# A hybrid attention and delta-rule encoder: the last attention norm step moved behind an inverse, four weight splits moved from GpSimd to VectorE

## The chip, the core and the metric

The kernel runs on one NeuronCore of a Trainium2 chip. The metric is the device time of one execution in microseconds (us). The engines are named as in the profile: PE is TensorE's matmuls and PEld its weight loads, DVE is VectorE, ACT is ScalarE, POOL is GpSimd, SP is the engine whose queue issues most transfers; ACT's queue issues some too. Each engine works through its own list of instructions in a fixed order that is set when the program is built.

## What is computed

The reference is a two-layer encoder over 1040 tokens (16 meta tokens and 1024 others) of width 1024. Each layer runs attention and a delta-rule recurrence on the same input, joins their outputs by one projection `w_out`, and goes on with a mixture of experts:

```python
y_att = _mla(...)                       # softmax attention, 4 heads, then an RMS norm per head
out = _rms_norm(out, out_norm.reshape(H_A, V_DIM))
...
def step(S, inp):                       # delta rule, forward and backward, 8 heads of 64
    r_t, w_t, k_t, v_t, kk_t, b_t = inp
    sa = jnp.einsum('bhvk,bhk->bhv', S, kk_t)
    S = S * w_t[:, :, None, :] - sa[..., None] * b_t[:, :, None, :] + v_t[..., None] * k_t[:, :, None, :]
    return S, jnp.einsum('bhvk,bhk->bhv', S, r_t)
...
mixed = jnp.concatenate([y_att, y_rwkv], axis=-1) @ w_out[li]
h = _layer_norm(DN_ALPHA * h + mixed, ln1_g[li], ln1_b[li])
```

## The kernel before

Each of the two layers runs through the same stages: projections, attention, delta rule, router, experts. The change lies at the seam from attention to delta rule, which the profiled execution passes at about 650 us (first layer) and 2260 us (second layer).

Attention ends with `normed` for the last of its four heads (the inner function at L883 to L907). It squares the head's output, sums it by a small matmul (L889), takes a power on POOL (L895), writes the 9x128 factors to DRAM (L897, SP queue), reads them back spread over all partitions as `rs` (L900, SP queue), multiplies (for the last head in one DVE instruction, L906, which waits for `rs`) and stores the normed head to `yatt_d` (L907, a transfer in ACT's queue).

The delta rule (function `rwkv`) cuts the sequence into 17 chunks of 64 and walks forward and backward at once; two steps, one of each direction, are a job. A job has four stages. Stage 0, `grams`, forms products on PE (L1509) that two engines take out of PSUM: `T` by DVE (L1514) and `AA` by ACT (L1515); the PSUM tile `e` has two buffers. Stage 1, `blocks`, inverts 16x16 blocks on DVE in 15 dependent steps of three small instructions (L1550, L1551, L1552), and spreads the result (L1558). Stage 2, `levels`, turns it (L1568, `X`), multiplies on PE (L1578, L1583), corrects and turns again on DVE (L1584, L1585) and finishes with two more products (L1592, L1599) that ACT takes out (L1595, L1602, `Y`). Stage 3, `chain`, is the recurrence: L1640 and L1647 need the state `ring`, L1658 needs `Y`, L1664 forms the next state. The tiles `ring` start as loads on the SP queue (L1611).

Beside this runs the generator `attended`, the projection of attention's output. It loads `w_out` in pieces kc of 128x1024 (L947, SP queue, into the tile `ht` with two buffers) and splits each into `wo_hi` (ACT, L209) and `wo_lo` (L212, on POOL). Then, token tile by token tile, it loads `yraw` from `yatt_d` (L959), splits it into `ya_hi` (ACT) and `ya_lo` (POOL), and runs 24 matmuls (L201 to L203) into PSUM tiles `e`, the same two buffers as stage 0. The order of all instructions on each engine is chosen by the scheduler of the tile framework from the order in which the code issues them; before, the first step of `attended` (the pieces kc 0 to 3) is issued ahead of the first job.

Of the kernel before, what the change touches and what calls it, by code (L numbers as in the profile page):

```python
# [170 lines left out]
def hybrid_encoder(ctx: ExitStack, tc: tile.TileContext, I, out):  # L171
# [184 lines left out]
    for li in range(DEPTH):  # L356
# [378 lines left out]
        with pool(tc, name="at", bufs=1, side="right") as at, pool(tc, name="ate", bufs=1, side="right") as even, \  # L735
# [147 lines left out]
            def normed(hd):  # L883

                sq = wk.tile([128, L], F32, name="p", bufs=5)
                nc.scalar.activation(sq, hd.yatt, AF.Square)
                ps = bank()
                for i, n, col in TILES:
                    nc.tensor.matmul(ps[:n, i:i + 1], sq[:, col:col + n], K("ones")[:, 0:1], start=True, stop=True)  # L889
                t = wk.tile([128, 2, NT + 1], F32, name="rmt")  # L890
                nc.vector.scalar_tensor_tensor(t[:, 0], hd.sums, 1e-6, hd.sums, op0=OP.mult, op1=OP.mult)
                for sl, n in ((slice(0, NT), 128), (slice(NT, NT + 1), META)):
                    nc.vector.scalar_tensor_tensor(t[:n, 0, sl], ps[:n, sl], 1.0 / 128, t[:n, 0, sl], op0=OP.mult,
                                                   op1=OP.add)
                nc.gpsimd.tensor_tensor(t[:, 1], t[:, 0], mhalf.to_broadcast([128, NT + 1]), op=OP.pow)  # L895
                rms_d = dram.tile([NT + 1, 128], F32, name="rms_d", bufs=2)
                nc.sync.dma_start(bass.AP(tensor=rms_d.tensor, offset=rms_d.offset, ap=[[1, 128], [128, NT + 1]]), t[:, 1])  # L897
                rs = wr_.tile([128, L], F32, name="rs", bufs=1)
                for c0, n, at_ in ((META, SEQ, 0), (0, META, SEQ)):
                    nc.sync.dma_start(rs[:, c0:c0 + n],  # L900
                                      bass.AP(tensor=rms_d.tensor, offset=rms_d.offset + at_, ap=[[0, 128], [1, n]]))
                if hd.h < 3:
                    nc.gpsimd.tensor_tensor(rs, hd.yatt, rs, op=OP.mult)
                    nc.gpsimd.tensor_scalar(rs, rs, P("on", hd.h), None, op0=OP.mult)
                else:
                    nc.vector.scalar_tensor_tensor(rs, hd.yatt, P("on", hd.h), rs, op0=OP.mult, op1=OP.mult)  # L906
                nc.scalar.dma_start(yatt_d[hd.h], rs)  # L907

            ahead = None
# [24 lines left out]
                    ahead = u  # L934
                before = hd
            values(ahead)
            normed(ahead.head)
        moe, mix = ExitStack(), ExitStack()
        rt = moe.enter_context(pool(tc, name=f"rt{li}", bufs=1))
        nt = NT if last else NT + 1  # L940
# [1 line left out]
        a_d = dram.tile([L, D], F32, name="a_d", tag="a_d", bufs=2)  # L942
        wo = {}

        def w_out(kc):
            raw = fp.tile([128, D], F32, name="ht", bufs=2)
            nc.sync.dma_start(raw, I["w_out"][li, :, kc])  # L947
            wo[kc] = pair(fp, [128, D], f"wo{kc % 4}")
            split(wo[kc], raw, None, nc.gpsimd)

        def attended(bank):


            for kc in range(4):
                w_out(kc)
            yield
            for i, n, col in TILES[:nt]:
                raw = fp.tile([128, 4, 128], F32, name="yraw")
                nc.sync.dma_start(raw[:, :, :n], yatt_d[:, :, col:col + n].rearrange("a p t -> p a t"))  # L959
                ya = pair(fp, [128, 4, 128], "ya")  # L960
                split(ya[:, :, :n], raw[:, :, :n], None, nc.gpsimd)
                ht = fp.tile([128, D], F32, name="ht", bufs=2)
                nc.sync.dma_start(ht[:n], h_rows[2 * li][row0(i):row0(i) + n])
                for j in range(2):
                    js = slice(j * 512, (j + 1) * 512)
                    ps = bank()
                    for kc in range(4):
                        mm3(ps[:n], ya[:, kc, :n], wo[kc][:, js], start=kc == 0, stop=kc == 3)
                    nc.vector.scalar_tensor_tensor(ht[:n, js], ht[:n, js], ALPHA, ps[:n], op0=OP.mult, op1=OP.add)
                    if j == 1:  # L970
                        nc.sync.dma_start(a_d[row0(i):row0(i) + n], ht[:n])
                    yield
            for kc in range(4, 8):
                w_out(kc)
            yield

            while True:
                if not ready:
                    yield
                    continue  # L980
                i = ready.pop(0)
                _, n, col = TILES[i]
                ya = pair(fp, [128, 4, 128], "ya")
                split(ya[:, :, :n], yTr[:, :, col:col + n], None, nc.gpsimd)
                ht = fp.tile([128, D], F32, name="ht", bufs=2)
                nc.sync.dma_start(ht[:n], a_d[row0(i):row0(i) + n])
                for j in range(2):
                    js = slice(j * 512, (j + 1) * 512)
                    ps = bank()
                    for kc in range(4):  # L990
                        mm3(ps[:n], ya[:, kc, :n], wo[4 + kc][:, js], start=kc == 0, stop=kc == 3)
                    nc.vector.scalar_tensor_tensor(ht[:n, js], ht[:n, js], 1.0, ps[:n], op0=OP.mult, op1=OP.add,
                                                   accum_out=sums[:n, i, j:j + 1])
                    if j == 1:
                        nc.sync.dma_start(a_d[row0(i):row0(i) + n], ht[:n])
                        done.append(i)
                    yield
# [1 line left out]
        ready, done = [], []  # L999
        sums = fp.tile([128, NT + 1, 2], F32, name="sums")  # L1000
        yTr = mix.enter_context(pool(tc, name="yr", bufs=1)).tile([128, 4, L], F32, name="yTr")
        finished, finish = rwkv(tc, li, last, K, P, pc, kr_d, bk_d, bon_d, g_dram, vt_d, yTr, mhalf, mix, attended, ready)

        tiles = [TILES[i] for i in finished]
        y_dst = y_rows[li]
# [440 lines left out]
                        tokens(e + 4)  # L1446


def rwkv(tc, li, last, K, P, pc, kr_d, bk_d, bon_d, g_dram, vt_d, yT, mhalf, kept, side, ready):

    nc = tc.nc
    V = nc.vector
# [79 lines left out]
    def blocks(As, E):  # L1532

        n = sum(A.shape[1] for A in As)
        dg = ws.tile([128, n, 16], F32, name="dg")
        at = []
        for A in As:
            U = A.shape[1]
            at.append(slice(at[-1].stop if at else 0, (at[-1].stop if at else 0) + U))
            tmp = ws.tile([128, U, 64], F32, name="tmp")  # L1540
            E.tensor_tensor(tmp, A, K("dg")[:, None, :].to_broadcast([128, U, 64]), op=OP.mult)
            E.tensor_tensor(tmp[:, :, 0:32], tmp[:, :, 0:32], tmp[:, :, 32:64], op=OP.add)
            E.tensor_tensor(dg[:, at[-1]], tmp[:, :, 0:16], tmp[:, :, 16:32], op=OP.add)  # L1543
        Y16 = ws.tile([128, n, 16], F32, name="Y16")
        V.tensor_copy(Y16, K("i16")[:, None, :].to_broadcast([128, n, 16]))
        sb = ws.tile([128, n, 16], F32, name="sb")
        for t_ in range(15, 0, -1):
            cs = slice(t_, 16)
            w = 16 - t_
            V.stream_shuffle(sb[:, :, cs], Y16[:, :, cs], [t_] * 16 + [16 + t_] * 16)  # L1550
            V.tensor_tensor(sb[:, :, cs], sb[:, :, cs], dg[:, :, t_:t_ + 1].to_broadcast([128, n, w]), op=OP.mult)  # L1551
            V.tensor_tensor(Y16[:, :, cs], Y16[:, :, cs], sb[:, :, cs], op=OP.subtract)  # L1552
        Ys = []
        for s in at:
            U = s.stop - s.start
            Y = wk.tile([128, U, 64], F32, name="Y", bufs=4)
            bd = K("bd16")[:, None, :].to_broadcast([128, U, 64])
            V.tensor_tensor(Y.rearrange("p c (b j) -> p c b j", b=4), Y16[:, s, None, :].to_broadcast([128, U, 4, 16]),  # L1558
                            bd.rearrange("p c (b j) -> p c b j", b=4), op=OP.mult)
            Ys.append(Y)  # L1560
        return Ys

    def levels(A, Y):

# [7 lines left out]
        for q0 in range(0, U, 8):  # L1572
# [9 lines left out]
                for s in HALF:  # L1582
                    nc.tensor.matmul(ps[s, u], W[s, q0 + u], Y[s, q0 + u], start=True, stop=True)  # L1583
            V.tensor_tensor(Y[:, q], Y[:, q], ps[:, :nq], op=OP.subtract)  # L1584
        V.transpose(X.rearrange(flat), Y.rearrange(flat))  # L1585

        cf, cg = slice(0, 32), slice(32, 64)
        fg = [(slice(base, base + 32), slice(base + 32, base + 64)) for base in (0, 64)]
# [11 lines left out]
                                 tile_position=(g.start, f.start))  # L1600
        for f, g in fg:
            nc.scalar.activation(Y[f, :, cg], ps[f, :U], AF.Copy, scale=-1.0)  # L1602

    orders = [list(range(NC)), list(range(NC - 1, 0 if last else -1, -1))]
    rings, touched, ends = {}, {}, []
# [114 lines left out]
    def stage(k, j):  # L1720
        if j < len(jobs):
# [4 lines left out]
            elif k == 1:  # L1726
                js = [0] if j == 0 else [x for x in (j, j + 1) if j % 2 and x < len(jobs)]
                if js:
                    Ys.update(zip(js, blocks([gs[x][1] for x in js], V if j == 0 else nc.gpsimd)))
            elif k == 2:  # L1730
                levels(gs[j][1], Ys[j])
            else:
                chain(job, gs.pop(j), Ys.pop(j))

    side = side(lambda: pe.tile([128, 512], F32, name="e"))
    next(side)
    for k, j in ((0, 0), (1, 0), (0, 1), (2, 0), (0, 2), (1, 1)):
        stage(k, j)
        if k == 0 and j == 1:
            for x in range(AHEAD):  # L1740
                new_ring(*steps[x])
# [34 lines left out]
```

## Time and profile before

| | us |
|---|---|
| median of 3 runs | 3237.86 |
| lowest and highest run | 3231.32, 3243.92 |
| profiled execution, its own time | 3243.99 |
| its span in the trace | 3242.1 |

The span is what the trace covers; 1.9 us of the execution's time lie around it, and the profiled execution is 6.1 us above the median. In the timeline rows below, the first number is the start in us from the span's start, the second the duration in us, then engine, line, operation, tiles and count; a bracket at the end holds the idle time of that engine just before the row and what ended it. In the trace a float32 matmul counts as two instructions.

### The profile page before, as it was taken

Reading aid. Unit: us, or ns where it says so; the run is one execution under the profiler, and the core shown is the slowest. Engines: PE = TensorE matmul, PEld = TensorE weight load, DVE = VectorE, ACT = ScalarE, POOL = GpSimd, SP = SyncE. Lnnn points to the kernel's source line nnn. Section 1 sums busy time; section 2 is a strip of 40 time slices with the busy share of each in tenths; the row PEclk is TensorE's granted clock in tenths of the full one; section 3 lists DMA queues with packets and bytes.
Section 4 is the critical chain, followed back from the end, with each engine's and each line's share of the span. In section 5 each row is a group of like instructions: output and inputs, shape, how many; then the busy total and the mean of one; then the engine's idle time right before and its main releaser. Section 6 shows DMA issues by size and latency. Waiting matters only on the chain. (4 is left out here: it accounts for less than half of the span.)

```text
span 3242.1 us, 57910 instructions
## 1 busy us (share of the span) xinstructions
PE 2737.0 (84%) x22160; PEld 2231.9 (69%) x22160; DVE 2174.9 (67%) x4257; ACT 1658.0 (51%) x3604; POOL 1040.8 (32%) x1049
## 2 busy tenths in 40 slices
PE   5989899979998978888498997999699889788882
PEld 4878687768776765666388876888587767566551
DVE  7667554566677668888656747445666666787885
ACT  5334454544445447777433435445344434577772
POOL 3656211143336411111245632112433544111111
PEclk9999899968978979999799988988787879799996
DMA  5345610233323449999724565102432325688875
GB/s 175 103 144 174 200 35 21 66 108 105 91 78 96 144 176 327 323 318 314 252 70 136 161 205 182 40 14 75 130 101 67 95 81 185 235 310 313 309 278 223
DMA packets 342732, 523.76 MB, mean 162 GB/s; under 512 B 110733, under 2 KB 263309, under 8 KB 315809
## 3 DMA queue, kind: packets, MB, share of 16 engines
q1 hardware_dynamic: 234832, 399.11, 38.2%
q10 hardware_dynamic: 93280, 87.04, 7.9%
q0 software_dynamic: 14336, 33.84, 2.9%
q8 instruction: 176, 2.88, 0.4%
q14 instruction: 108, 0.88, 0.1%
HBM read 406.57 MB, written 129.84 MB: 165 GB/s over the span
## 5 line engine op out<-in xcount | busy, mean ns | idle before, releaser
L1221 DVE TENSOR_TENSOR w_lo<-raw,w_hi 128x512 fp32r<-128x512 f32 x768 | 472.8, 684 | 9.3 <-ACT w_hi L1217 9.1
L1217 ACT ACTIVATE w_hi<-raw 128x512 fp32r<-128x512 f32 x768 | 412.1, 620 | 0.0
L201 PE MATMUL pj<-hT_hi,w_hi 128*128 128x352 f32 (+1 forms) x912 | 303.3, 333 | 3.7 <-ACT k L437 2.7
L202 PE MATMUL pj<-hT_lo,w_hi 128*128 128x352 f32 (+1 forms) x912 | 301.4, 331 | 2.8 <-DVE hT_lo L212 2.8
L203 PE MATMUL pj<-hT_hi,w_lo 128*128 128x352 f32 (+1 forms) x912 | 299.7, 329 | 0.0
L1273 POOL DMA_INDIRECT y_rows<-y,VS x64 | 64.5, 1007 | 617.6 <-ACT y L1272 595.7
L201 PE MATMUL ph<-w_hi,xT_hi 128*96 128x512 f32 x512 | 226.9, 443 | 3.4 <-ACT w_hi L1217 3.4
L202 PE MATMUL ph<-w_lo,xT_hi 128*96 128x512 f32 x512 | 222.7, 435 | 1.3 <-DVE w_lo L1221 1.3
L203 PE MATMUL ph<-w_hi,xT_lo 128*96 128x512 f32 x512 | 221.4, 432 | 0.0
L1509 PE MATMUL e<-T,BK 64*128 64x128 f32 x1072 | 171.8, 340 | 38.3 <-DMA T<-kr_d 21.0
L212 DVE TENSOR_TENSOR pT_lo<-tr,pT_hi 128x512 fp32r<-128x512 f32 (+2 forms) x176 | 101.4, 592 | 127.5 <-ACT pT_hi L209 127.0
L201 PEld LDWEIGHTS pj<-hT_hi,w_hi 128*128 128x128 f32 x912 | 176.6, 194 | 14.6 <-issue 6.9
L202 PEld LDWEIGHTS pj<-hT_lo,w_hi 128*128 128x128 f32 x912 | 176.6, 194 | 9.3 <-issue 4.9
L1509 PEld LDWEIGHTS e<-T,BK 64*128 64x128 f32 x1072 | 145.0, 234 | 54.1 <-ACT AA L1515 19.8
L203 PEld LDWEIGHTS pj<-hT_hi,w_lo 128*128 128x128 f32 x912 | 176.1, 193 | 5.0 <-issue 4.3
L1514 DVE TENSOR_TENSOR T<-e,cc 64x512 f32<-64x512 f32 x134 | 92.2, 688 | 89.3 <-PE e L1509 86.9
L1654 POOL TENSOR_TENSOR sp<-ring,pc 64x256 f32<-64x256 f32 x126 | 85.2, 676 | 165.9 <-DVE ring L1667 145.1
L209 ACT ACTIVATE pT_hi<-tr 128x512 fp32r<-128x512 f32 (+2 forms) x176 | 86.7, 517 | 94.3 <-PE tr L873 92.9
L1551 DVE TENSOR_TENSOR sb<-sb,dg 128x16 f32<-128x16 f32 (+8 forms) x270 | 107.1, 397 | 40.5 <-POOL dg L1543 33.4
L203 PEld LDWEIGHTS ph<-w_hi,xT_lo 128*96 128x96 f32 x512 | 93.1, 182 | 43.1 <-issue 3.2
L201 PEld LDWEIGHTS ph<-w_hi,xT_hi 128*96 128x96 f32 x512 | 93.4, 182 | 42.5 <-ACT w_hi L1217 4.1
L202 PEld LDWEIGHTS ph<-w_lo,xT_hi 128*96 128x96 f32 x512 | 93.1, 182 | 40.2 <-DVE w_lo L1221 2.3
(422 smaller groups left out, 7635.3 us busy)
## 6 DMA issues: line engine op xcount, KB each, us to landing
raw<-in_w_moe_dram SPq DMA_DIRECT2D x192, 1024.0 KB
w_raw<-in_w_in_dram SPq DMA_DIRECT2D x38, 512.0 KB
T<-kr_d SPq DMA_DIRECT2D x134, 128.0 KB
ys<-y_rows SPq DMA_DIRECT2D x16, 1024.0 KB
a_d<-ht SPq DMA_DIRECT2D x25, 512.0 KB
h_rows<-h ACTq DMA_DIRECT2D x24, 512.0 KB
kr_d<-KR ACTq DMA_DIRECT2D x16, 576.0 KB
bk_d<-BK ACTq DMA_DIRECT2D x16, 576.0 KB
```

The costliest lines, as they stand in the source:

```text
L201: nc.tensor.matmul(o, a.hi, b.hi, start=start, stop=False)
L202: nc.tensor.matmul(o, a.hi, b.lo, start=False, stop=False)
L203: nc.tensor.matmul(o, a.lo, b.hi, start=False, stop=stop)
L209: hi = nc.scalar.activation(dst.hi, src, AF.Copy)
L212: return hi, e_lo.tensor_tensor(dst.lo, src, dst.hi.bitcast(F32), op=OP.subtract)
L1217: nc.scalar.activation(w.hi[:, cs], raw[:, cs], AF.Copy)
L1221: V.tensor_tensor(w.lo[:, cs], raw[:, cs], w.hi[:, cs].bitcast(F32), op=OP.subtract)
L1273: nc.gpsimd.indirect_dma_start(out=rows, out_offset=bass.IndirectOffsetOnAxis(ap=vs, axis=0), in_=y[:n], in_offset=None, bounds_check=2 * ...
L1509: nc.tensor.matmul(ps[o][:, u], BK[h, q0 + u].rearrange("p a t -> p (a t)"), T[h, q0 + u, o], start=True, stop=True)
L1514: V.tensor_tensor(T[b, q, o], ps[o][b], mask[b, None, :].to_broadcast([64, 4, 128]), op=OP.mult)
L1551: V.tensor_tensor(sb[:, :, cs], sb[:, :, cs], dg[:, :, t_:t_ + 1].to_broadcast([128, n, w]), op=OP.mult)
L1654: nc.gpsimd.tensor_tensor(sp[a], ring[a, :, o], pc[a, d, :, c:c + 1].to_broadcast([64, 4, 64]), op=OP.mult)
```

## The change

In the last head, `normed` gives back its DVE instruction and its store. `rwkv` adds an ordering (no semaphore) that keeps the DVE instruction L906 behind the last L1552 of the first job's inverse. The first step of `attended` is issued after stage 2 of the first job, behind its second turn (L1585 of before), and the pieces kc 0 to 3 are split with DVE in place of POOL; pieces 4 to 7 stay on POOL.

```diff
-                    nc.vector.scalar_tensor_tensor(rs, hd.yatt, P("on", hd.h), rs, op0=OP.mult, op1=OP.mult)
+                    scaled = nc.vector.scalar_tensor_tensor(rs, hd.yatt, P("on", hd.h), rs, op0=OP.mult, op1=OP.mult)
+                    return scaled.ins, nc.scalar.dma_start(yatt_d[hd.h], rs).ins
                 nc.scalar.dma_start(yatt_d[hd.h], rs)
...
-            normed(ahead.head)
+            late = normed(ahead.head)
...
-        def w_out(kc):
+        def w_out(kc, E):
...
-            split(wo[kc], raw, None, nc.gpsimd)
+            split(wo[kc], raw, None, E)
...
             for kc in range(4):
-                w_out(kc)
+                w_out(kc, nc.vector)
...
             for kc in range(4, 8):
-                w_out(kc)
+                w_out(kc, nc.gpsimd)
...
-    next(side)
     for k, j in ((0, 0), (1, 0), (0, 1), (2, 0), (0, 2), (1, 1)):
-        stage(k, j)
+        last_ = stage(k, j)
+        if (k, j) == (1, 0):
+
+            tc.add_manual_dep(late[0], last_.name, mybir.DependencyInfo(
+                mybir.DependencyClass.NoSync, mybir.DependencyReason.DATA), reason="order")
+        if (k, j) == (2, 0):
+            with tc.issue_after(last_):
+                next(side)
```

The line numbers of the kernel after are larger by 1 in stages 0 to 2 (its L1553 is L1552 of before) and by 2 in stage 3 (its L1666 is L1664).

DVE, first layer, the end of the first job's inverse, before; `Y_6090` is the 16-column inverse, and L906 is the norm step:

```order
L1550 STREAM_SHUFFLE sb<-Y_6090 128x8x12
L1551 TENSOR_TENSOR sb<-sb,dg 128x8x12
L906 SCALAR_TENSOR_TENSOR rs<-yatt,cp,rs 128x1040
L1552 TENSOR_TENSOR Y_6090<-Y_6090,sb 128x8x12
L1550 STREAM_SHUFFLE sb<-Y_6090 128x8x13
L1551 TENSOR_TENSOR sb<-sb,dg 128x8x13
L1552 TENSOR_TENSOR Y_6090<-Y_6090,sb 128x8x13
```

The norm step stands inside step 12 of 15. The same place in the kernel after, from step 15 on; `X` is what stage 2 starts from:

```order
L1551 STREAM_SHUFFLE sb<-Y_6066 128x8x15
L1552 TENSOR_TENSOR sb<-sb,dg 128x8x15
L1553 TENSOR_TENSOR Y_6066<-Y_6066,sb 128x8x15
L906 SCALAR_TENSOR_TENSOR rs<-yatt,cp,rs 128x1040
L1559 TENSOR_TENSOR Y<-Y_6066,cc 128x512
L1569 STREAM_TRANSPOSE X<-Y 128x512
L1546 COPY Y_6373<-cc 128x256
L1551 STREAM_SHUFFLE sb<-Y_6373 128x16
L1515 TENSOR_TENSOR T<-e,cc 64x4x128 x2
L1585 TENSOR_TENSOR Y<-Y,m 128x512
L1586 STREAM_TRANSPOSE X<-Y 128x512
L212 TENSOR_TENSOR wo_lo<-ht,wo_hi 128x1024 x2
```

The norm step has moved behind step 15, but it still stands ahead of the spreading and of the first turn; two weight splits follow the second turn, and the other two come twelve rows later. In the second layer it stood between the second and the third instruction of step 15 before, and stands behind that step now.

ACT, first layer, from `W`, the result of the first product of stage 2, to `Y`, before:

```order
L1579 ACTIVATE W<-m 128x512
L209 ACTIVATE ya_hi<-yraw 128x512
L1524 ACTIVATE BK<-BK,pc 128x128
L1515 ACTIVATE AA<-e 64x512
L1524 ACTIVATE BK<-BK,pc 128x128 x3
L1515 ACTIVATE AA<-e 64x512
L1524 ACTIVATE BK<-BK,pc 128x128
L1515 ACTIVATE AA<-e 64x512
L1524 ACTIVATE BK<-BK,pc 128x128 x3
L1515 ACTIVATE AA<-e 64x512
L1595 ACTIVATE W<-m 32x8x32 x2
L1602 ACTIVATE Y<-m 32x8x32 x2
```

And after:

```order
L1580 ACTIVATE W<-m 128x512
L1525 ACTIVATE BK<-BK,pc 128x128
L209 ACTIVATE ya_hi<-yraw 128x512
L1516 ACTIVATE AA<-e 64x512
L1525 ACTIVATE BK<-BK,pc 128x128 x3
L1516 ACTIVATE AA<-e 64x512
L1525 ACTIVATE BK<-BK,pc 128x128 x4
L1516 ACTIVATE AA<-e 64x512
L1596 ACTIVATE W<-m 32x8x32 x2
L1516 ACTIVATE AA<-e 64x512
L209 ACTIVATE wo_hi<-ht 128x1024 x2
L1603 ACTIVATE Y<-m 32x8x32 x2
```

The split of the first token tile now stands ahead of one more pair of `AA` (before, two `AA` of that pair stood ahead of `W`), and the last two `wo_hi` stand between the two last results of stage 2.

SP, first layer, from the read of `rs` on, before; `ring` are the states, `ht` the pieces of `w_out`:

```order
L900 DMA rs<-rms_d 128x16
L1611 DMA ring<-vt_d 64x4x64 x3
L947 DMA ht<-in_w_out_dram 128x1024
L1611 DMA ring<-vt_d 64x4x64 x2
L947 DMA ht<-in_w_out_dram 128x1024
L1611 DMA ring<-vt_d 64x4x64 x7
```

And after:

```order
L900 DMA rs<-rms_d 128x16
L1613 DMA ring<-vt_d 64x4x64 x12
L1499 DMA BK<-bk_d 64x4x64 x2
L1496 DMA BK<-bk_d 64x512
L1499 DMA BK<-bk_d 64x4x64 x2
L960 DMA yraw<-yatt_d 128x4x128
L1701 DMA bg<-bon_d 128x4x128
L1702 DMA bg<-g_dram 128x4x128
L960 DMA yraw<-yatt_d 128x4x128
L948 DMA ht<-in_w_out_dram 128x1024 x2
```

The third and fourth piece have moved from among the state loads to behind the load of the second token tile. In the second layer the third piece stood ahead of all state loads before. On PE the first job's `Y` product (L1658 of before) stood behind 24 projection matmuls in the first layer and 17 in the second; after, it stands ahead of them, and 19 of the 24 stand between it and the next state (L1664 of before). By the fourth recurrence step PE has done the same work in both orders, but for one product.

## Rows read from the trace of the kernel before

**Rows 1.** Busy time of each engine by stretch of the span:
```profile
core 0: us, PE busy (x) PEld busy (x) DVE busy (x) ACT busy (x) POOL busy (x), PEclk, DMA share, GB/s
660.00:702.00 42.00, 25.26 (x252) 21.83 (x252) 29.66 (x76) 13.75 (x30) 21.36 (x24) 0.60 0.49 132
...
740.00:860.00 120.00, 113.16 (x1678) 94.17 (x1678) 84.74 (x221) 56.89 (x138) 44.75 (x53) 0.89 0.36 100
2268.00:2311.00 43.00, 22.55 (x232) 19.63 (x233) 24.97 (x73) 14.31 (x31) 22.27 (x25) 0.61 0.49 126
...
2360.00:2480.00 120.00, 112.89 (x1668) 94.29 (x1668) 76.90 (x199) 55.94 (x134) 44.73 (x53) 0.87 0.36 100
```

**Rows 2.** Waits of PE, 655 to 705 us: total us, times, longest:
```profile
PE tu L1640 <- DMA ring<-vt_d: 10.5, 1, 10.5
PE e L1509 <- ACT AA L1515: 2.4, 2, 1.9
PE m L1578 <- DVE X L1568: 2.0, 1, 2.0
PE m L1592 <- DVE X L1585: 1.5, 1, 1.5
```

**Rows 3.** Waits of PE, 2265 to 2315 us:
```profile
PE tu L1640 <- DMA ring<-vt_d: 16.4, 1, 16.4
PE e L1509 <- ACT AA L1515: 4.4, 2, 3.7
```

**Rows 4.** Timeline of DVE, first layer, the first job's inverse:
```profile
657.22 2.28 DVE L1552 TENSOR_TENSOR Y<-Y,sb 128x72 f32<-128x72 f32 x1
...
664.42 0.26 DVE L1551 TENSOR_TENSOR sb<-sb,dg 128x96 f32<-128x96 f32 x1
669.59 1.30 DVE L906 SCALAR_TENSOR_TENSOR rs<-yatt,cp,rs 128x1040 f32<-128x1040 f32 x1 [4.91 <-DMA ring<-vt_d]
...
676.88 0.71 DVE L1568 STREAM_TRANSPOSE X<-Y 128x512 f32<-128x512 f32 x1
```

**Rows 5.** Timeline of POOL, first layer, the splits of the first two pieces:
```profile
657.05 4.66 POOL L212 TENSOR_TENSOR wo_lo<-ht,wo_hi 128x1024 fp32r<-128x1024 f32 x2
```

**Rows 6.** Line L212 by engine and tile: shortest, median, longest in ns:
```profile
L212 POOL TENSOR_TENSOR wo_lo<-ht,wo_hi x16: 2332/2353/2576, 657.1 to 2595.4; 128x1024 fp32r<-128x1024 f32 x16
...
L212 DVE TENSOR_TENSOR wkv_lo<-yatt,wkv_hi x2: 1211/1218/1225, 355.2 to 1958.6; 128x1024 fp32r<-128x1024 f32 x2
```

**Rows 7.** Timeline of the SP queue, first layer:
```profile
669.69 0.55 SPq L947 DMA_DIRECT2D ht<-in_w_out_dram  x1
...
681.77 0.60 SPq L959 DMA_DIRECT2D yraw<-yatt_d  x1
```

**Rows 8.** Waits of the SP queue, 655 to 700 us:
```profile
SPq L1611 <- DMA yatt_d<-rs: 3.0, 1, 3.0
```

**Rows 9.** Timeline of ACT and its queue, first layer:
```profile
670.92 0.34 ACTq L907 DMA_DIRECT2D yatt_d<-rs  x1
...
675.84 1.06 ACT L209 ACTIVATE wo_hi<-ht 128x1024 fp32r<-128x1024 f32 x1 [1.43 <-DMA ht<-in_w_out_dram]
...
685.20 0.63 ACT L209 ACTIVATE ya_hi<-yraw 128x512 fp32r<-128x512 f32 x1 [1.57 <-DMA yraw<-yatt_d]
```

**Rows 10.** Timeline of PE, first layer, from the states to the first turn:
```profile
672.32 1.08 PE L1647 MATMUL y<-ring,T 128*64 128x64 f32 x14 [0.55 <-DMA ring<-vt_d]
673.85 1.77 PE L1509 MATMUL e<-T,BK 64*128 64x128 f32 x16 [0.45 <-ACT AA L1515]
677.65 1.98 PE L1578 MATMUL m<-X,tl 64*64 64x64 f32 x32 [2.02 <-DVE X L1568]
```

**Rows 11.** Timeline of the SP queue, DVE, PE and ACT, second layer:
```profile
2277.84 0.38 SPq L947 DMA_DIRECT2D ht<-in_w_out_dram  x1
...
2281.92 1.30 DVE L906 SCALAR_TENSOR_TENSOR rs<-yatt,cp,rs 128x1040 f32<-128x1040 f32 x1 [5.81 <-DMA ht<-in_w_out_dram]
...
2284.05 1.27 PE L1640 MATMUL tu<-ring,T 128*64 128x64 f32 x15 [16.44 <-DMA ring<-vt_d]
...
2294.12 0.63 ACT L209 ACTIVATE ya_hi<-yraw 128x512 fp32r<-128x512 f32 x1 [2.93 <-DMA yraw<-yatt_d]
```

More of the change, by code (lines that the diff above doesn't have):

```diff
@@ L1001, in hybrid_encoder @@
         yTr = mix.enter_context(pool(tc, name="yr", bufs=1)).tile([128, 4, L], F32, name="yTr")
-        finished, finish = rwkv(tc, li, last, K, P, pc, kr_d, bk_d, bon_d, g_dram, vt_d, yTr, mhalf, mix, attended, ready)
+        finished, finish = rwkv(tc, li, last, K, P, pc, kr_d, bk_d, bon_d, g_dram, vt_d, yTr, mhalf, mix, attended, ready, late)
         tiles = [TILES[i] for i in finished]
@@ L1446, in moe_layer, with rwkv @@
                         tokens(e + 4)
-def rwkv(tc, li, last, K, P, pc, kr_d, bk_d, bon_d, g_dram, vt_d, yT, mhalf, kept, side, ready):
+def rwkv(tc, li, last, K, P, pc, kr_d, bk_d, bon_d, g_dram, vt_d, yT, mhalf, kept, side, ready, late):
     nc = tc.nc
@@ L1551, in blocks @@
             V.tensor_tensor(sb[:, :, cs], sb[:, :, cs], dg[:, :, t_:t_ + 1].to_broadcast([128, n, w]), op=OP.mult)
-            V.tensor_tensor(Y16[:, :, cs], Y16[:, :, cs], sb[:, :, cs], op=OP.subtract)
+            done = V.tensor_tensor(Y16[:, :, cs], Y16[:, :, cs], sb[:, :, cs], op=OP.subtract)
         Ys = []
@@ L1560, in blocks @@
             Ys.append(Y)
-        return Ys
+        return Ys, done.ins
     def levels(A, Y):
@@ L1584, in levels @@
             V.tensor_tensor(Y[:, q], Y[:, q], ps[:, :nq], op=OP.subtract)
-        V.transpose(X.rearrange(flat), Y.rearrange(flat))
+        turned = V.transpose(X.rearrange(flat), Y.rearrange(flat))
         cf, cg = slice(0, 32), slice(32, 64)
@@ L1602, in levels @@
             nc.scalar.activation(Y[f, :, cg], ps[f, :U], AF.Copy, scale=-1.0)
+        return turned.ins
     orders = [list(range(NC)), list(range(NC - 1, 0 if last else -1, -1))]
@@ L1728, in stage @@
                 if js:
-                    Ys.update(zip(js, blocks([gs[x][1] for x in js], V if j == 0 else nc.gpsimd)))
+                    inverse, done = blocks([gs[x][1] for x in js], V if j == 0 else nc.gpsimd)
+                    Ys.update(zip(js, inverse))
+                    return done
             elif k == 2:
-                levels(gs[j][1], Ys[j])
+                return levels(gs[j][1], Ys[j])
             else:
```

## The prediction

> **What bounds the kernel now.** First the busy time by stretch [rows 1]: away from the seam PE is busy 113.16 of 120 us in the first layer and 112.89 of 120 in the second, at a granted clock near 0.88; in the two seams it is busy 25.26 of 42 us and 22.55 of 43, at 0.60 and 0.61. PE's work is not changed, and behind the fourth recurrence step it has the same order, so the change is worth what it takes from, or adds to, PE's idle time in these two stretches. The waits of PE say what ended them. In the first layer four waits count [rows 2]: 10.5 us for the states `ring`, 2.4 for PSUM tiles that `AA` holds, 2.0 and 1.5 for the two turns `X`, together 16.4. In the second layer the turns are not among them: 16.4 for `ring` and 4.4 for `AA` [rows 3], together 20.8. The timelines then show what stands behind each.
>
> **Part one, the norm step L906.** Before, it stood inside the inverse and DVE waited 4.91 us for `rs`, until 669.59 [rows 4]; steps 13 to 15 came behind it, and X was finished at 677.59 (676.88 + 0.71). One of those steps was also stretched by a split on POOL, as in part two. After, all 15 steps are done before the wait. But L906 still waits for `rs`, and spreading and first turn still stand behind it. From the same 669.59: 1.30 for L906, 0.8 for the spreading (an estimate, 512 columns like the turn), 0.71 for the turn, so X at 672.4, that is 5.2 us earlier. PE gets there at 673.4, since the last state loads end its L1647 only then (672.32 + 1.08) [rows 10]. The waits of 2.0 and 1.5 for X go; they are 3.5 us together. In the second layer L906 already stood in step 15 and no wait for X was late, so nothing is taken there.
>
> **Part two, the four splits.** A split of 128x1024 takes 2.35 us on POOL and 1.22 on DVE (the 1.22 is of another tile of the same size) [rows 6]. POOL is relieved of 4 x 2.35 = 9.4 us per layer and DVE takes on 4.9. While POOL's pair ran from 657.05 to 661.71 [rows 5], an inverse step of DVE that otherwise takes about 0.26 took 2.28 [rows 4]; these stretched steps vanish from the first inverse. They were hidden where DVE then waited for `rs`, and the one behind it is in the 5.2 above. The splits on DVE stand behind the second turn and inside the second job's inverse, whose result PE needs only some 25 us later. That cover hides them; without it, they cost up to 4.9 us per layer, less the stretching that goes.
>
> [...]
>
> **Part three, the transfers.** The third and fourth piece (512 KB each) leave the queue ahead of and among the state loads. In the first layer this changes nothing for the first state: `rs` and the first state are ahead of the piece that was issued at 669.69 [rows 7], and DVE's wait ended by the same moment [rows 4]. The 10.5 stays. In the second layer one piece was issued at 2277.84, ahead of every state, `rs` came at 2281.92 and the first state at 2284.05 [rows 11]. The state can't come much before `rs`, which is issued first, so the gain lies between 0 and 2.1; I take 1.9, and the wait becomes 14.5.
>
> **What is new, first: ACT's order.** `ya_hi` needs `yraw`, which needs the store L907. It now stands ahead of the `AA` pair whose PSUM tiles PE wants next. In the first layer the states' transfer queue waited 3.0 us for that store [rows 8], which was issued at 670.92 [rows 9]; after, it stands behind one more copy on ACT, about 0.8 us later, and so are `yraw` (issued at 681.77 before [rows 7]) and the end of `ya_hi`: 685.20 + 0.63 + 0.8 = 686.6 [rows 9], and the first `AA` behind it about 0.5 later, 687.1. PE meanwhile: free at 673.4, first product 1.98, a group of L1509 between 1.77 at that stage and 3.6 if it waits inside, the second product as long as the first, 1.98 [rows 10]. That is 679.1 to 680.9, and then PE waits 6.2 to 8.0 us; I take 7.2. Before, this stretch had 2.4 us of such a wait [rows 2], while `ya_hi` waited 1.57 [rows 9] with two more `AA` done. So what X gains is given back here, behind the transfer. In the second layer `ya_hi` started at 2294.12 [rows 11]. Two transfer issues ahead of `yraw` are gone (0.38 and about 0.55), the store is later by up to 0.8, and PE arrives 1.9 earlier; I take 3.2 for the `AA` wait, against 4.4 before [rows 3], between 2.7 and 5.1.
>
> **What is new, second: the last two `wo_hi`.** On ACT they stand ahead of `Y`, and PE needs `Y` for the next states. Their pieces are issued behind the second `yraw`, which waits until `ya_lo` has read the first. From 686.6, with about 1.3 for `ya_lo` (half of a POOL split of twice the size) and two or three issues of 0.6, the second piece is issued near 689.7. The piece issued at 669.69 was taken up at 675.84, 6.15 later [rows 7, 9]. So 695.8, with 1.06 for one `wo_hi` [rows 9] and 0.8 for `Y` 697.7. PE's own products behind 687.1 (two groups of L1509, two small products, one product of the chain: about 10 us by the same durations) reach to 697. I take 1.0 us per layer, between 0 and 6. The loads of residual rows that follow on the SP queue now wait for the two late splits; nothing that PE wants within 20 us stands behind them.
>
> **The sum.** First layer: 16.4 before; 10.5 + 7.2 + 1.0 = 18.7 after, +2.3, with ends at -3.5 (only the turns' waits go) and +8. Second layer: 20.8 before; 14.5 + 3.2 + 1.0 = 18.7 after, -2.1, ends -5 and +5. Together +0.2. The profiled execution took 3243.99 us (span 3242.1, 1.9 around it), 6.1 over the median of 3237.86; +0.2 makes 3244.2 of it and 3238 of the median.
>
> **The rivals.** *No wait behind the transfer (A).* If `yraw` lands early enough, as the shorter queue speaks for, neither new wait comes: the first layer goes from 16.4 to 10.5, the second from 20.8 to 14.5 + 3.2, so 5.9 + 3.1 = 9 us are gained, 3229. Against it: `yraw` followed its issue by 3.4 us [rows 7, 9], and that issue hangs on the store.
>
> *The granted clock rises earlier (B), faster.* PE's clock is 0.60 in these stretches [rows 1]. If the broken-up waits let it run at 0.88, 25.26 x (1 - 0.60/0.88) = 8.0 and 22.55 x (1 - 0.61/0.87) = 6.7 us are saved; with the 5.2 of the earlier X that is 19.9, 3218. Against it: the longest waits, 10.5 and 14.5, stay where they are, and a new one of 7 is put in.
>
> *POOL held up by DVE's splits (C).* The mechanism of the stretched row, turned round: each split holds a POOL step 1.22 us. Of 9.8 us in both layers about half would fall on steps that `ya_lo` or the next inverse needs: +4.9, 3243.
>
> *ACT's queue blocked by late pieces (D), slower.* ACT takes its list in order [rows 9]; a piece that lands late holds `Y`, and behind it every `AA`. This decides once a piece takes over about 10 us instead of 6.15 to be taken up: residual rows, `bg` and `BK` then share the queue with it, and the seam's DMA share is 0.49 already [rows 1]. At 15 us it costs 9 in each layer, 3238 + 18 = 3256. [...]
>
> **How the numbers follow.** About 0.5%, 16 us, is what a measurement of this kernel can tell from no change. Forecast 3238: 0.54; A 3229: 0.15; C 3243: 0.10; these three lie within 0.5%, together 0.79. B 3218: 0.11, faster. D 3256: 0.10, slower. For the range I leave out half or more of B and D: 3222 to 3252. The ends of the sum (-8.5 and +13) lie inside it.
>
> **What would show it.** Right: L906 behind step 15 and still ended by `rs`; X near 672 and 2285; PE's wait for `ring` 10.5 and about 14.5; a wait of some 7 us (first layer) and 3 (second) for `AA`, with ACT idle before `ya_hi` on `yraw` at that time; DVE's splits near 1.22; `Y` behind a `wo_hi` that waits for its piece; the clock near 0.6 in both stretches. Wrong: no `AA` wait over 3 us in the first layer (A), a clock of 0.7 or more there (B), POOL steps stretched beside DVE's splits (C), or a wait of 5 us or more for `Y` (D).

## The result: 0.8% slower, and not in the seam

The kernel after takes 3265.94 us (median of 6 runs, 3261.39 to 3279.75), the kernel before 3240.89 in 6 runs beside it; the ratio is 1.008 with a 95% interval of 1.0055 to 1.0106. In a second set, on 12 runs of the kernel after, it is 1.0048 (1.0025 to 1.0071). The forecast was 3238 with a range of 3222 to 3252: the time lies 14 us above the range.

Both traces are cut at the same four places, the last norm product of attention and the first and the last state product (L1664 of before, L1666 of after) of each layer:

| stretch | before, us | after, us | difference |
|---|---|---|---|
| up to attention's last norm product | 652.8 | 657.7 | +4.9 |
| first seam | 51.3 | 47.6 | -3.7 |
| first recurrence | 398.0 | 418.3 | +20.3 |
| up to the second seam | 1160.3 | 1155.6 | -4.7 |
| second seam | 51.5 | 50.3 | -1.2 |
| second recurrence | 399.3 | 406.0 | +6.7 |
| rest | 528.9 | 529.1 | +0.2 |

The first and the fourth stretch have the same instructions in the same order at their start and end and cancel; a second profile of the kernel after has 647.9 and 1163.1 there. The seams gained 4.9 us. The recurrences, which the prediction took as unchanged, lost 27.0 between these two profiles.

Busy time of PE by stretch, of after (length, PE busy with its count, granted clock, DMA share, GB/s; the seams answer to [rows 1]):

```profile
657.70:705.30 47.60, 31.99 (x294) 0.61 0.53 138
705.30:1123.60 418.30, 374.37 (x5539) 0.83 0.31 88
2279.20:2329.50 50.30, 31.63 (x280) 0.59 0.51 129
2329.50:2735.50 406.00, 361.43 (x5331) 0.82 0.31 89
```

The two recurrences of before, in the same view:

```profile
704.10:1102.10 398.00, 364.99 (x5534) 0.86 0.34 96
...
2313.90:2713.20 399.30, 360.03 (x5326) 0.83 0.32 92
```

Idle time is length less busy time. PE was idle for 33.0 and 39.3 us in the recurrences of before and is idle for 43.9 and 44.6 in those of after, 16.2 us more. The rest of the 27.0 is busy time, 9.4 us more in the first, where the granted clock is 0.83 and was 0.86, and 1.4 more in the second, where it is 0.82 and was 0.83.

What PE waits for in the first recurrence, before (us in total, times, longest):

```profile
PE e L1509 <- DMA T<-kr_d: 10.0, 7, 2.5
PE y L1647 <- DVE yt L1674: 5.6, 4, 3.2
PE e L1509 <- ACT AA L1515: 5.4, 6, 2.6
```

And after:

```profile
PE y L1649 <- DVE yt L1676: 8.6, 4, 2.8
PE e L1510 <- ACT AA L1516: 6.5, 5, 2.5
PE e L201 <- ACT AA L1516: 4.8, 3, 2.3
...
PE e L1510 <- DMA T<-kr_d: 3.2, 3, 1.5
PE m L1593 <- DVE sb L1551: 2.8, 1, 2.8
...
PE e L201 <- DVE sb L1552: 2.2, 1, 2.2
```

Six of the 13 rows of the whole list of after are new. Products of the projection (L201) now stand in PE's queue ahead of the moment at which ACT or DVE frees their PSUM tile, and `m` products stand ahead of DVE's inverse steps. The waits for `T`, a load, are shorter in return. No edited instruction stands in this stretch; the crossed kernels below show that these waits go with the order of the instructions.

The orders say the same. Counted over the whole program, 4242 of 16354 matmuls stand at another place in the queue than before. Most of them stand in the two recurrences: of what is issued there behind the first turn of the loop over jobs, 3568 of 5812 matmuls, 864 of 1149 DVE instructions and 428 of 830 ACT instructions have another place (counted in the two tables of order that the crossed kernels below hold). PE has done the same work by the fourth step, as the text ahead of the prediction says, but from there on the two orders part again and again.

### The profile page after: what moved, and what is told of

The parts are those of the page before. It is cut to its first block, busy times and chain, and to the rows that moved or that the text cites. A ratio compares the mean times of both kernels' runs of the same rounds, so it can differ in the third digit from the quotient of the medians.

```text
span 3264.6 us, 57911 instructions
## 1 busy us (share of the span) xinstructions
PE 2743.4 (84%) x22160; PEld 2237.5 (69%) x22160; DVE 2181.7 (67%) x4265; ACT 1655.3 (51%) x3604; POOL 1024.5 (31%) x1041
## 5 line engine op out<-in xcount | busy, mean ns | idle before, releaser
L201 PE MATMUL pj<-hT_hi,w_hi 128*128 128x352 f32 (+1 forms) x912 | 303.8, 334 | 3.7 <-ACT k L437 2.7
L201 PE MATMUL ph<-w_hi,xT_hi 128*96 128x512 f32 x512 | 224.4, 438 | 3.4 <-ACT w_hi L1218 3.4
L212 DVE TENSOR_TENSOR pT_lo<-tr,pT_hi 128x512 fp32r<-128x512 f32 (+2 forms) x176 | 101.2, 592 | 128.9 <-ACT pT_hi L209 128.2
L201 PEld LDWEIGHTS pj<-hT_hi,w_hi 128*128 128x128 f32 x912 | 177.2, 194 | 14.4 <-issue 7.1
L201 PEld LDWEIGHTS ph<-w_hi,xT_hi 128*96 128x96 f32 x512 | 92.7, 181 | 42.0 <-ACT w_hi L1218 3.8
L203 PEld LDWEIGHTS ph<-w_hi,xT_lo 128*96 128x96 f32 x512 | 92.0, 180 | 42.2 <-issue 2.6
L421 POOL TENSOR_SCALAR w_hi<-w_raw 128x1024 fp32r<-128x1024 f32 x34 | 102.3, 3010 | 56.6 <-PE pj L202 56.6
```

Source lines behind the costliest of these rows:

```text
L201: nc.tensor.matmul(o, a.hi, b.hi, start=start, stop=False)
L203: nc.tensor.matmul(o, a.lo, b.hi, start=False, stop=stop)
L212: return hi, e_lo.tensor_tensor(dst.lo, src, dst.hi.bitcast(F32), op=OP.subtract)
L421: nc.gpsimd.tensor_scalar(w.hi, wr, 1.0, None, op0=OP.mult)
```

## The experiments

Two theories were put against each other. **Order:** the scheduler, which lays out all that follows from a small edit, made a new order for both recurrences, and that order idles more. **Seam:** the new seam leaves something behind (late splits, DVE's load, a lower clock) that slows the recurrence, whatever its order.

### The two parts crossed

The recurrence's order can be held. Everything that is issued from the second turn of the loop over jobs on is tied, engine by engine, to the instruction that stood ahead of it in a chosen kernel, by ordering edges without semaphores. So the new seam can be run with the old order, and the old seam with the new one.

```diff
     for j in range(len(jobs)):
+        if j == 1:
+            first_ = len(nc.cur_bb.bb.instructions)
...
     for _ in range(6):
         next(side)
+    pinned(tc, ORDER.get(li, {}), nc.cur_bb.bb.instructions[first_:])
...
+        for a, b in zip(line, line[1:]):
+            tc.add_manual_dep(b, a.name, mybir.DependencyInfo(
+                mybir.DependencyClass.NoSync, mybir.DependencyReason.DATA), reason="order")
```

`line` is one engine's instructions in the chosen order, read from a table in the kernel. The new seam with the old order:

> The change as it is, but from the second turn of the loop over jobs on, each engine's instructions of the recurrence are held in the order in which they stood in the kernel before. Order theory (the time is lost because the scheduler laid out the whole recurrence anew): the two seams keep the 3.7 and 1.2 us that they gained, the recurrences lose the 20.3 and 6.7 us again, so about 3236 us, 5 below the kernel before. Seam theory (the recurrence is slow because of what the new seam leaves behind: later splits, DVE's extra work, a lower clock): the order doesn't matter, 3260 to 3266 us. Mixed: 3245 to 3255.

The old seam with the new order, the same edit on the kernel before:

> The kernel before, with nothing of the change, but from the second turn of the loop over jobs on, each engine's instructions of the recurrence are held in the order in which they stand in the kernel after. Order theory: 3241 + 20.3 + 6.7 = about 3268 us. Seam theory: no change, 3236 to 3246 us.

The kernel after, beside them:

> The kernel after once more, to see whether the stages lose the same time in a second profile: both theories 3262 to 3269 us; the first layer's recurrence about 20 us longer than before, the second's about 7 longer, if the loss belongs to the program; split otherwise, if a large part of it is scatter of the clock.

Measured in one set, with 3249.14 us for the kernel before: new seam with old order 3243.36 (ratio 0.9979, 0.9955 to 1.0003), old seam with new order 3262.68 (1.0046, 1.0022 to 1.007), kernel after 3262.62. The old order takes back the loss though every edit of the change is in it; the new order makes a loss though none is. The second part fell short: 13.5 us above before, where 27 were expected. No kernel was run with the edges and its own order, but both crossed kernels have the edges, and only the one with the new order is slower.

The recurrences of the new seam with the old order:

```profile
705.50:1106.10 400.60, 370.50 (x5539) 0.86 0.33 95
2310.00:2721.50 411.50, 372.79 (x5332) 0.80 0.31 89
```

Idle 30.1 and 38.7 us, as in the kernel before, at 411.5 us and a clock of 0.80 in the second layer. Of the old seam with the new order:

```profile
705.60:1107.20 401.60, 359.27 (x5534) 0.87 0.33 93
2321.90:2730.60 408.70, 364.61 (x5326) 0.81 0.31 90
```

Idle 42.3 and 44.1, as in the kernel after, but at a clock of 0.87 in the first layer, against 0.83, so that the first recurrence isn't longer here than with the old order. The new waits go with the order: on the old seam, with the new order, the first recurrence has (line numbers are shifted by the code that holds the order; L204 is L201 of before, L1525 is L1509)

```profile
PE e L204 <- ACT AA L1531: 4.8, 3, 2.3
...
PE e L1525 <- DMA T<-kr_d: 2.9, 3, 1.5
```

and on the new seam, with the old order, PE's list has no wait at L204, and the wait for `T` is long again:

```profile
PE e L1526 <- DMA T<-kr_d: 9.0, 8, 2.0
```

Of the kernel after once more:

```profile
695.60:1113.70 418.10, 374.15 (x5540) 0.83 0.31 88
2324.10:2729.00 404.90, 357.31 (x5331) 0.84 0.31 90
```

The first recurrence repeats to 0.2 us, idle time (43.9) and clock included, though attention before it ended 9.8 us earlier: this length belongs to the program.

Both crossed kernels were run a second time:

> The new seam with the old order once more. Order theory: again 3 to 9 us below before; PE's idle time in the two recurrences again 30 and 39 us within 2. If the first result was scatter of the runs: at or above before.

> The old seam with the new order once more. Order theory: again 10 to 18 us above before, idle 42 and 44 us in the two recurrences within 2. What is lost to the clock in the first recurrence was 47 us in the first profile against 64 in both profiles of the kernel after; if that is scatter, it may come anywhere from 45 to 65, if it belongs to the program, at 47 within 3.

With 3243.57 us for before: 3245.67 (1.0003, 0.9977 to 1.0028) and 3265.35 (1.0056, 1.003 to 1.0082). The loss by the new order stands, 21.8 us this time, more than the 10 to 18 that were expected. The gain of the new seam under the old order doesn't: the two ratios lie on both sides of 1. The recurrences, first with the old order on the new seam:

```profile
703.40:1107.30 403.90, 373.01 (x5540) 0.85 0.33 94
2310.90:2714.40 403.50, 363.87 (x5332) 0.83 0.31 90
```

and with the new order on the old seam:

```profile
709.70:1111.00 401.30, 358.11 (x5533) 0.87 0.32 93
2319.80:2735.80 416.00, 370.07 (x5326) 0.80 0.31 88
```

Idle 30.9 and 39.6, against 43.2 and 45.9. The clock of the first recurrence is 0.87 again with the new order on the old seam, against 0.83 twice in the kernel after: what is lost to the clock (an estimate from these rows: busy time times what the clock is short of 1) is about 47 us there and about 64 in the kernel after, and both repeat. As far as two profiles of each can tell, the clock of this stretch depends on seam and order together, while its idle time goes by the order.

One more profile of the kernel before completes the four:

> The kernel before in a second profile. PE's idle time in the two recurrences, if it belongs to the order, is again 33 and 39 us within 2; what is lost to the clock there (52 and 62 us) may differ by 10, as between the two kernels with the old order.

```profile
708.90:1112.40 403.50, 374.19 (x5534) 0.84 0.33 95
2328.20:2733.60 405.40, 367.50 (x5327) 0.81 0.32 90
```

Idle 29.3 and 37.9 us; the first is 3.7 below the first profile, a little more than expected, and the clock is 2 hundredths lower in both layers. The two recurrences together last 808.9 us here, 11.6 more than in the first profile of before, so part of the 27.0 above was scatter of the clock: against this profile the second one of after is 14.1 longer. This execution took 3266.14 us, at the upper end of what the kernel before takes. Over the four profiles of each order the idle time is 29.3 to 33.0 and 37.9 to 39.6 us with the old one, 42.3 to 43.9 and 44.1 to 47.6 with the new one: the means differ by 12.5 and 6.7, 19.2 together. Not all of this is length: with the new order the two recurrences are busy 6.9 us less in the mean and last 12.3 longer. In the first one on the old seam the clock makes up for all of it (401.6 and 401.3 us, against 398.0 to 403.9 with the old order). That the order costs time is shown by the medians over all runs; how the cost divides between idle time and clock is not settled. The medians differ by the order by 13.5 and 21.8 us on the old seam and by 19.3 on the new one (3262.62 against 3243.36).

### The old order in the first layer alone

The table is cut to the first layer.

```diff
 ORDER = {
     0: {
...
-    1: {
...
```

> The change as it is, with the recurrence of the first layer alone held in the order of before; the second layer keeps the new order. Order theory: PE's idle time in the first layer's recurrence falls from 43.9 us (measured twice in the kernel after) to 30 to 33, in the second it stays at 44 to 48 against 39 before; the time lies between that of the new seam with both old orders (6 us below before) and that of the kernel after (13 above): about 2 above before, since the first layer had most of the loss. Seam theory: like the kernel after, 13 above before.

3248.52 us against 3247.24 (1.0005, 0.9981 to 1.0028), 1.3 above before. The recurrences:

```profile
704.00:1109.40 405.40, 375.60 (x5539) 0.84 0.33 93
2315.00:2722.40 407.40, 363.06 (x5332) 0.82 0.31 89
```

Idle 29.8 in the layer with the old order, 44.3 in the one with the new. The order theory gave the second number and the time, and the first within 0.2; the seam theory gave 13 us, and the interval leaves that out.

### Parts of the change alone

Only the norm step is moved; the projection's first step is back ahead of the first job, its splits on POOL (against the kernel after):

```diff
-                w_out(kc, nc.vector)
+                w_out(kc, nc.gpsimd)
...
+    next(side)
     for k, j in ((0, 0), (1, 0), (0, 1), (2, 0), (0, 2), (1, 1)):
...
-        if (k, j) == (2, 0):
-            with tc.issue_after(last_):
-                next(side)
```

> Only the norm step is moved; the first step of the projection stays ahead of the first job with its splits on POOL. The scheduler lays the recurrence out anew here too (some 3200 of 16354 matmuls stand at another place, of 4242 in the kernel after). Order theory: the time moves by 10 us or more against before, to either side, though the seam's waits move by at most 5. Seam theory: 3236 to 3241 us, since DVE and POOL carry no more work than before behind the seam.

3259.47 us against 3249.14 in the medians, but single runs take from 3234.02 to 3280.42, and the ratio is 1.0013 (0.9982 to 1.0044): neither theory's number is shown. The recurrences:

```profile
699.80:1118.70 418.90, 382.13 (x5502) 0.82 0.31 88
2335.40:2741.90 406.50, 368.69 (x5326) 0.81 0.31 90
```

Idle 36.8 and 37.8: a third order costs some 6 us of idle time in the first layer; the rest of what its 418.9 us are longer comes with a clock of 0.82, against 0.86 and 0.84 in the two profiles of before.

Only the splits are on DVE:

```diff
-        if (k, j) == (1, 0):
-
-            tc.add_manual_dep(late[0], last_.name, mybir.DependencyInfo(
-                mybir.DependencyClass.NoSync, mybir.DependencyReason.DATA), reason="order")
-        if (k, j) == (2, 0):
-            with tc.issue_after(last_):
-                next(side)
...
+    next(side)
```

> Only the four splits are on DVE in place of POOL; the norm step and the first step of the projection stay where they were. Order theory: the scheduler lays the second layer's recurrence out anew nearly throughout, and the first's in its last third, so PE's idle time there is what that order makes of it and not what DVE's 4.9 us per layer cost; -5 to +15 us against before. A theory that DVE's load is what slows the recurrence: the same loss of 10 to 15 us as in the kernel after, in both layers, idle time in the first layer near 44.

3240.24 us against 3247.24 (0.9988, 0.9969 to 1.0008), 7 us below where -5 to +15 was expected. The recurrences:

```profile
703.80:1096.50 392.70, 360.79 (x5533) 0.88 0.34 97
2311.90:2709.60 397.70, 354.23 (x5325) 0.85 0.32 91
```

DVE's 4.9 us per layer slow nothing here: the recurrences are the shortest of all runs. In the second layer, whose order is new nearly throughout, PE idles 43.5 us, and yet the clock of 0.85 makes up for it. So a new order isn't bad as such, and more idle time isn't by itself more time.

Only the projection's first step is issued later, on POOL, without the norm step's edge:

```diff
-                w_out(kc, nc.vector)
+                w_out(kc, nc.gpsimd)
...
-            tc.add_manual_dep(late[0], last_.name, mybir.DependencyInfo(
-                mybir.DependencyClass.NoSync, mybir.DependencyReason.DATA), reason="order")
```

> Only the first step of the projection is issued later, behind the first job's second turn, with its splits on POOL and the norm step free. The scheduler's order changes least here of all parts: some 1200 of 16354 matmuls stand elsewhere, nearly all in the second half of the first layer's recurrence, almost none in the second layer's. Order theory: the second layer's recurrence idles as before (38 to 40 us), the first within 5 of before; the time within 8 us of before. Theory that the later pieces of the weights slow the recurrence: 10 us or more slower.

3240.92 us against 3247.24 (0.9987, 0.9962 to 1.0012). The recurrences:

```profile
707.20:1105.70 398.50, 367.74 (x5533) 0.85 0.34 96
2313.80:2719.70 405.90, 367.69 (x5326) 0.81 0.32 90
```

Idle 30.8 and 38.2, as the order theory had it; pieces of `w_out` that come later do no harm that shows.

### A seam that waits less

In the kernel after the first inverse is done 6 us (first layer) before `rs` lands and lies idle behind it. So, with the old order held, three more moves: the first two states are loaded ahead of `rs`, the norm step goes behind the first turn and its store behind the first `W`, and `ya_hi` goes behind `Y`.

```diff
+            for x in late[1]:
+                behind(x, state[3])
...
+        if (k, j) == (2, 0):
+            behind(late[0], last_[0])
+            with tc.issue_after(last_[1]):
+                next(side)
+            out = last_[2]
+            behind(late[2], last_[3])
...
+            if j:
+                next(side)
+            else:
+                with tc.issue_after(out):
+                    next(side)
```

`behind(a, b)` adds the ordering edge; `late[1]` are the two reads of `rs`, `state[3]` is the last load of the first two states, and `last_` holds the first turn, the second turn, `Y` and the first `W`.

> New seam with the recurrences held in the old order, and three more moves in the seam: the first two states' loads stand ahead of the read of rs in the SP queue, the norm step stands behind the first turn (its store behind the first W on ACT), and ya_hi stands behind Y on ACT. In the kernel after PE waits 10.9 and 14.4 us for the states and 4.6 and 3.8 for AA, though the inverse is done 6 and 9 us before rs lands. If the seam's waits are worth their length, the seams (47.6 and 50.3 us in the kernel after) shorten by 6 to 10 us each and the time comes to 10 to 20 us below before. If the wait only moves (to AA, to Y or to the projection's first products, which need ya), the seams stay within 3 us and the time is that of the new seam with the old order, 6 below before.

3239.71 us against 3243.57 (0.9976, 0.9944 to 1.0008). Once more:

> The states' loads ahead of the read of rs, with the old order, once more. In its first profile the seams lasted 38.8 and 46.7 us (51 and 52 in the kernel before), but 5 us of the work that PE did there before was done behind them, so some 8 us are left: 4 to 12 us below before. If the first result was scatter: within 3 us of before.

3238.40 against 3245.00 (0.9975, 0.9945 to 1.0005). Both times some 0.25% below before, and both intervals just reach 1. PE's waits in the first seam, first profile:

```profile
PE tu L1661 <- DMA ring<-vt_d: 8.0, 1, 8.0
PE e L1527 <- ACT AA L1533: 4.0, 2, 2.3
PE m L1601 <- ACT W L1597: 0.7, 1, 0.7
```

The wait for the states fell only to 8.0: in the SP queue the third of their four loads waits 6.2 us for `rms_d<-rmt`, the transfer that writes what `rs` is read from. The seams lasted 38.8 and 46.7 us, but part of their work now comes behind them, and so do new waits for `X`, 3.0 us in the first layer and 2.4 in the second. In the second recurrence PE idles 42.2 and 41.1 us in the two profiles, more than the 37.9 to 39.6 of the old order elsewhere. It is the version that comes closest to a gain over before, by about as much as can just be told.

## Why the prediction was wrong, step by step

**The step that failed** is the first: "behind the fourth recurrence step it has the same order, so the change is worth what it takes from, or adds to, PE's idle time in these two stretches". PE's work done by that step was compared, and from equal work an equal order was concluded for all that follows. The orders of all five engines part again. The new one, with no part of the change in the seam, slows the kernel by 13.5 and 21.8 us in the medians, and the old one takes the loss away on the new seam (19.3); PE idles 12.5 and 6.7 us more in the two recurrences under the new order, part of which the clock gives back. No rival had it: all four, D with its slower end included, lay in the seam.

**The seam itself** went much as forecast. PE's waits there, after, first layer:

```profile
PE tu L1642 <- DMA ring<-vt_d: 10.9, 1, 10.9
PE e L1510 <- ACT AA L1516: 4.6, 1, 4.6
```

and second layer:

```profile
PE tu L1642 <- DMA ring<-vt_d: 14.4, 1, 14.4
PE e L1510 <- ACT AA L1516: 3.8, 2, 3.0
PE m L1579 <- DVE X L1569: 0.5, 1, 0.5
```

They answer to [rows 2] and [rows 3]. The first layer's sum is 15.5, not 18.7. The second's is 18.7, as forecast, but by luck: a wait for `X` and a longer one for `AA` stand in for the 1.0 of the late `wo_hi`. The second profile of after has 10.8 and 4.8, and 15.3, 2.9 and 0.6.

*L906 and X:* right. DVE after, first layer, with `rs` landing 5.2 us later in this execution than before:

```profile
674.80 1.30 DVE L906 SCALAR_TENSOR_TENSOR rs<-yatt,cp,rs 128x1040 f32<-128x1040 f32 x1 [6.04 <-DMA ring<-vt_d]
...
676.73 0.71 DVE L1569 STREAM_TRANSPOSE X<-Y 128x512 f32<-128x512 f32 x1
```

X is finished 2.6 us behind the landing, where it was 8.0 before [rows 4]; 2.8 was forecast. PE's waits for X of 2.0 and 1.5 in the first layer are gone; the second layer has a new one of 0.5.

*States:* right, 10.9 for 10.5 and 14.4 for 14.5.

*`ya_hi` ahead of `AA`:* the wait came, at its place, but 4.6 for 7.2. SP and ACT, first layer:

```profile
682.14 0.60 SPq L960 DMA_DIRECT2D yraw<-yatt_d  x1
```

```profile
685.26 0.63 ACT L209 ACTIVATE ya_hi<-yraw 128x512 fp32r<-128x512 f32 x1 [4.62 <-DMA yraw<-yatt_d]
...
692.82 2.00 ACT L209 ACTIVATE wo_hi<-ht 128x1024 fp32r<-128x1024 f32 x2
```

From the landing of `rs`, `yraw` is issued 7.3 us later, where it was 12.2 before [rows 4, 7]. The term put it 0.8 later with the store; in fact the queue ahead of it is shorter by the two pieces, and its wait of 3.0 for the store [rows 8] is gone. In the second layer 3.8 came for 3.2, but most of it from another cause: DVE's pair of splits (below) held up `T`, and `AA` with it: `T` started at 2313.38, right behind the pair, and ACT was idle for 2.37 before its `AA`, until `T` came. In the second profile the foreseen cause is there: 2.9, behind an ACT that waits 2.13 for `yraw`.

*The late `wo_hi`:* no cost, where 1.0 per layer was put. The pieces, issued at 687.72, were there when ACT came to them.

**The rivals.** A, no wait behind the transfer: no, 4.6 came. B, the clock rises in the seam: no, 0.61 and 0.59. C, DVE's splits hold POOL, put at 1.22 per split by an estimate from [rows 6]: seen once, in the second layer of the first profile of after, where two POOL steps take 1.0 us more each and DVE's pair 1.5. D, late pieces block ACT: no.

## What to carry to other kernels

Where a scheduler sets the order, an edit can change the order of all that comes later, and the forecast has to compare the orders to the end, on every engine, not up to where the work done is equal again. A new order that falls out of an edit may be slower, as here, or do no harm, as with the splits alone: hold the old order by explicit edges behind the edited stage before judging the edit, and cross the two to see which of them has the time. Here the edit alone is worth too little to be measured, and the order that came with it cost 14 to 22 us.

## What the runs showed of the hardware

**The granted clock was 0.50 for 20 us while PE was busy without a gap, and 1.00 in another execution.** At the same place of the recurrence, which starts with the same products on PE, the kernel before has

```profile
846.00:866.00 20.00, 18.47 (x325) 1.00 0.48 135
```

and the kernel after

```profile
846.00:866.00 20.00, 20.00 (x186) 0.50 0.16 39
```

PE is busy without a gap at a granted 0.50 and does 186 instructions where the other does 325 at 1.00. But this doesn't tell the two kernels apart: in its second profile the kernel before has 0.50 there too.

```profile
844.90:848.90 4.00, 4.00 (x38) 0.50 0.14 33
848.90:852.90 4.00, 4.00 (x49) 0.50 0.02 6
```

Some us before this place PE waits for a load of `T`: 1.70 us in the first profile of before, whose clock stayed at 1.00, 2.03 in the second and 1.49 in the kernel after, whose clocks fell to 0.50. So the wait alone doesn't decide it. What does is open.

The new order's 0.83 on the new seam and 0.87 on the old differ most at one place, where the kernel after has

```profile
897.30:901.30 4.00, 4.00 (x71) 0.50 0.01 2
```

and the old seam with the new order

```profile
897.60:901.60 4.00, 4.00 (x38) 1.00 0.19 48
```

The clock of 0.50 lasts from 896.7 to 917.1 in the first, and no stretch at 0.50 falls between 862.6 and 917.2 in the second. The second profiles of both agree: 0.50 from 887.6 to 903.6 in that of the kernel after, whose recurrence starts 9.7 us earlier, and 1.00 from 869.7 to 917.7 in that of the old seam with the new order. Why is open.

**A pair of DVE splits and two POOL steps that ran side by side were both longer, by 1.5 us and by 1.0 each.** In the second layer of the kernel after the pair of splits took

```profile
2309.53 3.82 DVE L212 TENSOR_TENSOR wo_lo<-ht,wo_hi 128x1024 fp32r<-128x1024 f32 x2
```

where the first layer's pair took 2.32, and POOL beside it

```profile
2310.56 1.71 POOL L1522 TENSOR_TENSOR AA<-AA,cc 128x256 f32<-128x256 f32 x1
2312.23 2.25 POOL L1542 TENSOR_TENSOR tmp<-AA,cc 128x512 f32<-128x512 f32 x1
```

where the same steps of the first layer took 0.72 and 1.28; they began at 687.95 there, 2.4 us behind the end of the pair. That is the stretch of [rows 4, 5] with the roles changed: each POOL step is longer by 1.0 us, a little less than the 1.16 of one split. In the second profile of after the same pair takes 2.32 and the same POOL steps 0.73 and 1.28: neither is longer there.
